# Row loads, small fills, a head pass and a last update, moved between engines in a hybrid decoder layer

## The chip, the cores and the metric

One core of one Trainium2 chip. The metric is the device time of one execution of the whole layer, in microseconds (us). The kernel before took 931.19 us, the median of three runs (928.84 to 931.49). Five engines run side by side, each through its own stream of instructions: TensorE (PE; its weight loads are shown apart, as PEld), VectorE (DVE), ScalarE (ACT), GpSimd (POOL) and SyncE (SP). SP issues DMAs only; ScalarE and GpSimd issue some too.

## The reference

One decoder layer over x of 1 x 512 x 1024 in float32. Two SwiGLU feed-forward blocks stand around a token mixer; each block is normed ahead and after.

```
x = x + 0.5 * rms_norm(swiglu_ffn(rms_norm(x, pre[0]), ffn1_w_in, ffn1_w_out), post[0])
mixed = token_mixer(rms_norm(x, pre[1]), w_mix_in, ...)     # HGRN2 heads and mLSTM heads
x = x + rms_norm(mixed, post[1])
x = x + 0.5 * rms_norm(swiglu_ffn(rms_norm(x, pre[2]), ffn2_w_in, ffn2_w_out), post[2])

def rms_norm(x, g):  return x * rsqrt(mean(x * x, axis=-1) + 1e-6) * g
def swiglu_ffn(x, w_in, w_out):
    gate, up = split(x @ w_in, 2)                           # 1024 -> 2 x 2816
    return (silu(gate) * up) @ w_out                        # 2816 -> 1024
```

The mixer reads one combined projection `h @ w_in`; its first four head tiles of 128 columns are the forget gates of the HGRN2 heads.

## The kernel before, in words

The 512 tokens are four tiles of 128 (i = 0 to 3), kept in `xs` (128 partitions x 4 x 1024). Every matmul operand is split into a high and a low part: ScalarE copies a float32 tile to fp32r (the high part, L289), VectorE subtracts it from the original (the low part, L291). A product is three passes: high weights by high x (0), high by low (1), low by high (2). Weights come by DMA in tiles of 512 KB into rings of raw buffers, a planner giving each load the product at whose split it is issued.

The stages in order of time: the start (0 to about 23 us), where x is loaded, normed and transposed; the first feed-forward, ended by `ffn_out` and `last`; the mixer, opened by `head4`; the second feed-forward; the stores.

**The start** (`layer`, `warm`, `gain_row`, `gain_pe`, `start`, `root_whole`) is traced under `manual_schedule`, so each engine keeps the written order there. L1903 loads x in halves of 256 KB: the second halves of tiles 0 and 1 from ScalarE's queue, all others from SP's. The norm row `norm_pre[0]` (2 KB in each half) is loaded by L176 into partition 0 of `self.row`, which lies in `hf`, after L171 has zeroed that half on VectorE. `gain_pe` (L183) spreads the row over the 128 partitions with a matmul by ones. `warm` and `spin` (L189) keep TensorE busy ahead of that. `root_whole` takes a tile's squares on ScalarE (L726) and the root on Pool (L727, and `pow` at L728). VectorE then multiplies by the row (L746) and by the root (L749), or both at once (L741). The results are transposed on TensorE (L359), copied by ScalarE (L379), and the first product (L614 in `prod`) begins. At L1910 ScalarE runs a tiny Exp, so that its table is loaded early.

**Small parameters** (`small_params`) follow the start in the source: among them are three Pool memsets, of `gb` (L1278, into which a DMA puts the gate biases), `tiny` (L1284) and `one` (L1286). Outside `manual_schedule` the framework orders each engine's stream itself by priority and dependencies; `with self.behind(a)` makes what is traced in its block on a's engine follow a. A PSUM bank is one of eight `ps` buffers; `holes` takes four without using them.

**The mixer's head** (`head4`, `head_mm`): `last` computes the last four chunks of the first feed-forward's output (L997), norms each (`post1`) and goes on to the mixer's pre-norm. `head4` splits weight tiles 0 to 3 and norms tiles 2 and 3 between them; then `head_mm` runs one weight tile over tokens 0 to 255 (L554, 24 matmuls: three passes of 8), and `trans(2)` and `trans(3)` (L359, then copies at L365 and L366) follow the second and the third tile. After the fourth, `forget_gates` runs the same four tiles over tokens 256 to 511 (L544).

**The end** (`last`, `post1`, `store`): for tile i, `post1` takes squares on ScalarE (L448), the root r on Pool (L449, L453), multiplies by the post-norm gain on VectorE (L496), and adds y * r and late * r to the two halves of `xs` on VectorE (L504). `store` writes each half from SP's queue (L1893).

Of the kernel before, what the change touches and what calls it, by code (L numbers as in the profile page):

```python
# [10 lines left out]
AF = mybir.ActivationFunctionType  # L11
ALU = mybir.AluOpType
PSUM = bass.MemoryType.PSUM

P = 128
T = 512
D = 1024
FF = 2816
NT = T // P
ND = D // P  # L20
# [4 lines left out]
HALF = T // 2  # L25
# [7 lines left out]
TINY = 1e-37  # L33
# [85 lines left out]
class Layer:  # L119
# [53 lines left out]

    def gain_row(self, row, h):
        v = slice(512 * h, 512 * h + 512)
        self.nc.sync.dma_start(self.row[0:1, v], row[:, v])  # L176

    def gain_pe(self):

# [309 lines left out]
    def post1(self, i, y, parts, rms, pieces, g, out=None):  # L489

        nc = self.nc
        for ps, v in pieces:
            parts.append(ps)
            next(rms)
            o = ps if out is None else out[:, v]
            nc.vector.tensor_tensor(o, ps, g[:, 512 + v.start : 512 + v.stop], op=ALU.mult)  # L496
        r = next(rms)

        late = (1, pieces[0][0] if out is None else out)
        turned, added = out is None and i == NT - 1, None  # L500
        for h, v in (late, (0, y)) if turned else ((0, y), late):
            x = self.xs[:, i, 512 * h : 512 * h + 512]
            with self.behind(*[added] * (turned and added is not None)):
                added = nc.vector.scalar_tensor_tensor(x, v, r, x, op0=ALU.mult, op1=ALU.add)  # L504
        self.added = [self.square, added]
# [40 lines left out]
                    start=k + n + m == 0, stop=k == ND - 1 and n == 2, skip_group_check=True,  # L546
                )

    def head_mm(self, w):

        ps = self.ps()
        for m, (a, b) in enumerate(((0, 0), (0, 1), (1, 0))):
            for k in range(ND):
                self.nc.tensor.matmul(  # L554
                    ps[:, :HALF], w[:, a, k, :], self.xop(k, b, 0, HALF), start=m + k == 0, stop=m == 2 and k == ND - 1
                )
        self.head.append((w, ps))

    def head4(self, trans, scaled):

        self.head = []
        lows = [self.low]
        self.full_split()
        with self.behind(*lows, self.low):
            scaled(2, 0)
        with self.behind(self.added[0]):
            self.full_split()
            with self.behind(self.low):  # L570
                scaled(2, 1)
            self.full_split()
        scaled(3, 0)
        scaled(3, 1)
        with self.behind(self.normed[1]):
            self.feed()
        for n in range(4):
            self.head_mm(self.pull())
            if n in (1, 2):
                trans(1 + n)  # L580

    def open_ffn(self, ctx, second=False):

# [137 lines left out]
    def root_whole(self, i):  # L721

        nc = self.nc
        out = self.hf[:, 2 * i : 2 * i + 2, :].rearrange("p a t -> p (a t)")
        ss, m, r = self.col(), self.col(), self.col()
        nc.scalar.activation(out, self.xs[:, i, :], AF.Square, accum_out=ss)  # L726
        nc.gpsimd.tensor_scalar(m, ss, 1.0 / D, EPS, op0=ALU.mult, op1=ALU.add)  # L727
        nc.gpsimd.tensor_tensor(r, m, self.nhalf[:, :1], op=ALU.pow)  # L728
        return r

    def start(self, gpre):
# [518 lines left out]
    def small_params(self):  # L1250

        nc = self.nc
        mc = self.cp
        rows = self.sp.tile([36, P], F32, tag="junk", bufs=1, name="rows")
        nc.sync.dma_start(rows[0:16, :], self.conv_w[0].rearrange("j (c p) -> (j c) p", p=P))
        nc.sync.dma_start(rows[16:20, :], self.conv_b[0].rearrange("(c p) -> c p", p=P))
        nc.sync.dma_start(rows[20:28, :], self.hgrn_lb_logits.rearrange("r (c p) -> (r c) p", p=P))
        nc.sync.dma_start(rows[28:32, :], self.hgrn_norm[0].rearrange("(c p) -> c p", p=P))
        nc.sync.dma_start(rows[32:36, :], self.mlstm_norm[0].rearrange("(c p) -> c p", p=P))
        pt = self.ps()  # L1260
        nc.tensor.transpose(pt[:, :36], rows, self.ident[:36, :36])
        nc.vector.tensor_copy(self.prm, pt[:, :36])
        l0, l1 = self.prm[:, 20:24], self.prm[:, 24:28]
        mx, e0, e1 = self.col(4), self.col(4), self.col(4)
        nc.vector.tensor_tensor(mx, l0, l1, op=ALU.max)
        nc.vector.tensor_tensor(e0, l0, mx, op=ALU.subtract)
        nc.vector.tensor_tensor(e1, l1, mx, op=ALU.subtract)
        nc.scalar.activation(e0, e0, AF.Exp)
        nc.scalar.activation(e1, e1, AF.Exp)
        nc.vector.tensor_tensor(e1, e0, e1, op=ALU.add)  # L1270
        nc.vector.reciprocal(e1, e1)
        self.lb = mc.tile([P, 4], F32, name="lb")
        nc.vector.tensor_tensor(self.lb, e0, e1, op=ALU.mult)
        self.oml = mc.tile([P, 4], F32, name="oml")
        nc.vector.tensor_scalar(self.oml, self.lb, -1.0, 1.0, op0=ALU.mult, op1=ALU.add)

        self.gb = mc.tile([36, 1], F32, name="gb")
        nc.gpsimd.memset(self.gb, 0.0)  # L1278
        bias = self.mlstm_gate_bias[0].rearrange("(g h) -> g h", g=2)
        for g in range(2):  # L1280
            nc.sync.dma_start(self.gb[32 * g : 32 * g + 4, :], bias[g].rearrange("(h o) -> h o", o=1))

        self.tiny = mc.tile([P, 1], F32, name="tiny")
        nc.gpsimd.memset(self.tiny, TINY)  # L1284
        self.one = mc.tile([P, 1], F32, name="one")
        nc.gpsimd.memset(self.one, 1.0)  # L1286

    def masks(self, mc, mb):

# [566 lines left out]
def layer(tc, aps):  # L1856
    with ExitStack() as ctx:
        L = Layer(ctx, tc, aps)
        nc = tc.nc
        x, out = aps["x"], aps["out"]  # L1860
        pre, post = aps["norm_pre"][0], aps["norm_post"][0]
        L.weights(
            L.ffn_items("f1", aps["ffn1_w_in"][0], aps["ffn1_w_out"][0]) + L.mix_items()
            + L.ffn_items("f2", aps["ffn2_w_in"][0], aps["ffn2_w_out"][0])
        )
        gp, xn, roots = [None], [None] * NT, {}

        def norm(i, row=None):
            if i == 0 and row is not None:
                gp[0] = L.gain("gpre", pre[row : row + 1, :])  # L1870
            xn[i] = L.pre(i, gp[0], row == 2 and i == NT - 1)

        def root(i):

            if i < 2:
                norm(i, 1)
            else:
                roots[i] = L.root(i)

        def scaled(i, h):  # L1880
            r, xn[i] = roots[i]
            L.scaled(i, gp[0], r, xn[i], h)

        def trans(i):
            L.to_t(i, xn[i])

        def trans_s(i):
            L.to_s(i, xn[i])

        def store(i):  # L1890
            for h in range(2):
                v = slice(512 * h, 512 * h + 512)
                nc.sync.dma_start(out[0, i * P : (i + 1) * P, v], L.xs[:, i, v])  # L1893

        with ExitStack() as f1:
            L.open_ffn(f1)
            with tc.manual_schedule():
                first = L.start_loads()
                L.warm()
                for i in range(NT):  # L1900
                    for h in range(2):
                        v = slice(512 * h, 512 * h + 512)
                        (nc.scalar if i < 2 and h else nc.sync).dma_start(L.xs[:, i, v], x[0, i * P : (i + 1) * P, v])  # L1903
                    if i < 2:
                        L.gain_row(pre[0:1, :], i)
                    if i:
                        L.load(first.popleft())
                    if i == 1:

                        nc.scalar.activation(L.col(), L.nhalf[:, :1], AF.Exp)  # L1910
                while first:
                    L.load(first.popleft())
                gp[0] = L.cp.tile([P, D], F32, tag="gpre", bufs=1, name=L.nm("gpre"))
                L.start(gp[0])
            L.small_params()
            L.ffn_in()
            L.ffn_out(post[0:1, :], 0.5, root, trans, lambda trans: L.head4(trans, scaled))
        L.mixer()
        with ExitStack() as f2:
            L.open_ffn(f2, True)  # L1920
            L.mix_out1(lambda i: norm(i, 2), trans_s, L.ffn_head)
            L.ffn_in()
            L.ffn_out(post[2:3, :], 0.5, store, lambda i: None, lambda trans: None)
# [30 lines left out]
```

## Time and profile before

| What | us |
|---|---|
| Median of three runs | 931.19 (928.84 to 931.49) |
| The profiled execution | 929.26 |
| Its span, first to last instruction | 927.6 |
| TensorE matmul busy | 917.6 |
| VectorE busy | 766.7 |
| ScalarE busy | 524.3 |
| GpSimd busy | 183.4 |

The profiled execution is one run; the profile's times count from the start of its span, and 1.66 us of its time lie outside the span. In a timeline row stand start, length, engine, source line, operation, output and inputs with their shapes, how many instructions the row merges (x), and in brackets the idle time of the engine just before, with what ended it. SPq and ACTq are DMA issues on those engines' queues. q1 in the DMA rows is SP's ring, q10 ScalarE's. The granted clock of TensorE was 0.999 of full speed.

### The profile page before, as it was taken

What the parts mean: (1) busy time and instruction counts of PE and PEld (TensorE: products, weight loads), DVE (VectorE), ACT (ScalarE), POOL (GpSimd) and SP (SyncE); (2) the same over time, 40 slices, a digit from 0 to 9 for tenths busy, and PEclk for the clock granted to TensorE, in tenths of its full rate; (3) what the DMA queues carried; (4) which work ended last, traced back from release to release, by engine and by line L of the source; (5) the groups of instructions that cost most, each with busy time, mean ns of one, the idle gap of its engine ahead of it and who ended that gap; (6) DMA issues with size and microseconds to landing.
All of it is one profiled execution on the core that took longest, in us unless ns stands there. A gap on an engine that the chain in (4) does not pass through costs nothing.

```text
span 927.6 us, 18301 instructions
## 1 busy us (share of the span) xinstructions
PE 917.6 (99%) x7425; PEld 883.9 (95%) x7425; DVE 766.7 (83%) x994; ACT 524.3 (57%) x751; POOL 183.4 (20%) x252
## 2 busy tenths in 40 slices
PE   8999999999999999999999999999999999999997
PEld 7999999999999999998888887899999999999997
DVE  6899988889887876698767555699898889998885
ACT  7645455557566466956533345595354545756661
POOL 2431112111111046652220310314000000011002
PEclk9999999999999999999999999999999999999999
DMA  9255878766897824898832124262354435278542
GB/s 315 73 165 131 190 206 197 191 151 159 222 282 226 246 79 131 170 196 185 171 75 70 46 92 155 96 183 70 113 160 137 137 115 160 93 218 259 174 144 92
DMA packets 118768, 145.42 MB, mean 157 GB/s; under 512 B 7414, under 2 KB 91418, under 8 KB 118684
## 3 DMA queue, kind: packets, MB, share of 16 engines
q1 hardware_dynamic: 102716, 129.05, 45.2%
q0 software_dynamic: 15680, 14.69, 12.0%
q8 instruction: 58, 0.95, 0.4%
q10 hardware_dynamic: 288, 0.52, 0.2%
q14 instruction: 26, 0.21, 0.1%
HBM read 142.14 MB, written 31.46 MB: 187 GB/s over the span
## 4 chain that ended last, share of the span: by engine, by line
PE 59%; DVE 2%; DMA 1%; issue 1%; ACT 1%; POOL 0%; DVEq 0%; POOLq 0%; ACTq 0%
PE ps L614 19%; PE ps L1005 8%; PE ps L544 6%; PE ps L193 5%; PE ps L195 5%; PE ps L194 5%; PE ps L997 4%; PE ps L1423 2%; DMA raw<-in_ffn_w_in_dram 1%; DVE w L291 1%; PE ps L359 1%; PE ps L554 1%; PE ps L1516 0%; PE ps L1721 0%; PE ps L1694 0%
## 5 line engine op out<-in xcount | busy, mean ns | idle before, releaser
L289 ACT CAST w<-raw 128x1024 fp32r<-128x1024 f32 x246 | 251.1, 1027 | 196.4 <-PE ps L614 95.8
L291 DVE TENSOR_TENSOR w<-raw,w 128x1024 fp32r<-128x1024 f32 x246 | 299.3, 1220 | 30.6 <-ACT w L289 28.5
L614 PE MATMUL ps<-xq,w 128*128 128x256 f32 x2016 | 237.1, 277 | 0.0
L614 PEld LDWEIGHTS ps<-xq,w 128*128 128x128 f32 x2016 | 232.9, 188 | 0.0
L614 PE MATMUL ps<-sq,w 128*128 128x256 f32 x1512 | 178.0, 276 | 0.6 <-DVE ps L633 0.3
L614 PEld LDWEIGHTS ps<-sq,w 128*128 128x128 f32 x1512 | 174.3, 188 | 1.4 <-ACT ps L665 0.9
L305 DVE TENSOR_TENSOR raw<-raw,raw 128x1024 f32<-128x1024 f32 x72 | 89.9, 1252 | 8.1 <-DMA raw<-in_ffn_w_in_dram 6.6
L1005 PE MATMUL ps<-w,hs 128*128 128x256 f32 x672 | 81.0, 276 | 0.0
L997 PE MATMUL ps<-w,hs 128*128 128x256 f32 x672 | 79.2, 276 | 0.0
L1005 PEld LDWEIGHTS ps<-w,hs 128*128 128x128 f32 x672 | 78.4, 188 | 0.0
L193 PE MATMUL ps<-w,xq 128*128 128x512 f32 x192 | 77.9, 407 | 0.1
L997 PEld LDWEIGHTS ps<-w,hs 128*128 128x128 f32 x672 | 77.5, 188 | 0.0
L194 PE MATMUL ps<-w,xq 128*128 128x512 f32 x192 | 74.8, 391 | 0.0
L195 PE MATMUL ps<-w,xq 128*128 128x512 f32 x192 | 74.8, 391 | 0.0
L544 PE MATMUL ps<-xq,w 128*128 128x256 f32 x480 | 55.8, 277 | 0.0
L544 PEld LDWEIGHTS ps<-xq,w 128*128 128x128 f32 x480 | 54.9, 188 | 0.5 <-issue 0.5
L937 POOL DMA_DIRECT2D f2sums<-in_ffn_w_out_dram x15 | 20.3, 1502 | 176.9 <-DMA f2sums<-in_ffn_w_out_dram 176.6
L877 ACT CAST hs<-hf 128x1024 fp32r<-128x1024 f32 x32 | 33.7, 1053 | 28.9 <-PE ps L1005 21.2
L878 DVE TENSOR_TENSOR hs<-hf,hs 128x1024 fp32r<-128x1024 f32 x32 | 39.1, 1222 | 8.8 <-ACT hs L877 8.2
L193 PEld LDWEIGHTS ps<-w,xq 128*128 128x128 f32 x192 | 36.1, 188 | 8.4 <-issue 1.0
L937 POOL DMA_DIRECT2D f1sums<-f1sums x26 | 22.3, 857 | 110.2 <-DMA f1sums<-in_ffn_w_out_dram 58.2
L195 PEld LDWEIGHTS ps<-w,xq 128*128 128x128 f32 x192 | 36.0, 188 | 8.1 <-DVE xq L366 0.3
(275 smaller groups left out, 1215.8 us busy)
## 6 DMA issues: line engine op xcount, KB each, us to landing
raw<-in_ffn_w_in_dram SPq DMA_DIRECT2D x98, 512.0 KB, 5.5
raw<-in_ffn_w_out_dram SPq DMA_DIRECT2D x44, 512.0 KB, 4.5
raw<-in_w_mix_in_dram SPq DMA_DIRECT2D x28, 512.0 KB, 5.9
raw<-f2sums SPq DMA_DIRECT2D x15, 512.0 KB
raw<-f1sums SPq DMA_DIRECT2D x13, 512.0 KB, 7.0
raw<-in_w_mix_out_dram SPq DMA_DIRECT2D x8, 512.0 KB, 3.8
f2sums<-in_ffn_w_out_dram SPq DMA_DIRECT2D x30, 128.0 KB, 6.3
f2sums<-in_ffn_w_out_dram SPq DMA_DIRECT2D x15, 256.0 KB, 4.5
```

The costliest lines, as they stand in the source:

```text
L193: mm(ps, sh, mh, start=start, stop=False, **kw)
L194: mm(ps, sh, ml, start=False, stop=False, **kw)
L195: mm(ps, sl, mh, start=False, stop=stop, **kw)
L289: nc.scalar.copy(hi, raw)
L291: self.low = nc.vector.tensor_tensor(lo, raw, hi.bitcast(F32), op=ALU.subtract)
L305: added = (nc.vector if late else nc.gpsimd).tensor_tensor(o, o, c, op=ALU.add)
L544: mm(ps[:, u0:u1], w[:, a, k, :], self.xop(k, b, u0, u1), start=k + n + m == 0, stop=k == ND - 1 and n == 2, skip_group_check=True,)
L614: self.nc.tensor.matmul(ps[:, c], wb[b][:, k, v], left[d][:, k, :], start=first and a + n + k == 0, stop=n == 2 and k == KH - 1, skip_grou ...
L878: self.nc.vector.tensor_tensor(lo, src, hi.bitcast(F32), op=ALU.subtract)
L937: nc.gpsimd.dma_start(to[:, a:b], v, accum_op=ALU.add)
L997: mm(out, a[kk][:, i * P : (i + 1) * P], w[:, b, kk, QUARTER * v : QUARTER * (v + 1)], start=begin and c == kk == n == 0, stop=kk == 1 and ...
L1005: mm(ps[:, QUARTER * c : QUARTER * (c + 1)], A[a][:, c], B[b], start=begin and c == n == 0, stop=n == 2, skip_group_check=True,)
```

## The change

Four edits. **Rows:** the two norm-row DMAs are issued from ScalarE's queue; row 0 is traced ahead of x, row 1 after x[1]. The second half of x[0] moves to SP's queue, so that ScalarE's holds row 0, the second half of x[1], row 1. **Fills:** the three Pool memsets of `small_params` stand behind the `pow` of the start's last root. **Head:** `head_pass` does one pass of one tile, and the third tile's pass 0 is run between the second tile's passes 1 and 2; `trans(2)` still follows the second tile's last pass and `trans(3)` the third's. **Last update:** for the last token tile of the second feed-forward, ScalarE multiplies the upper 256 columns of `out` by r, VectorE updates columns 0 to 511 and 512 to 767, and Pool adds columns 768 to 1023; that tile is stored in three pieces, the last of them from ScalarE's queue.

```diff
     def gain_row(self, row, h):
         v = slice(512 * h, 512 * h + 512)
-        self.nc.sync.dma_start(self.row[0:1, v], row[:, v])
+        self.nc.scalar.dma_start(self.row[0:1, v], row[:, v])
...
         late = (1, pieces[0][0] if out is None else out)
+        if self.second and out is not None and i == NT - 1:
+            x = self.xs[:, i, :]
+            nc.scalar.activation(out[:, 256:], out[:, 256:], AF.Copy, scale=r)
+            for a, b, v in ((0, 512, y), (512, 768, out[:, :256])):
+                nc.vector.scalar_tensor_tensor(x[:, a:b], v, r, x[:, a:b], op0=ALU.mult, op1=ALU.add)
+            nc.gpsimd.tensor_tensor(x[:, 768:], x[:, 768:], out[:, 256:], op=ALU.add)
+            return
...
-    def head_mm(self, w):
-
-        ps = self.ps()
-        for m, (a, b) in enumerate(((0, 0), (0, 1), (1, 0))):
-            for k in range(ND):
-                self.nc.tensor.matmul(
-                    ps[:, :HALF], w[:, a, k, :], self.xop(k, b, 0, HALF), start=m + k == 0, stop=m == 2 and k == ND - 1
-                )
-        self.head.append((w, ps))
+    def head_pass(self, t, m):
+
+        if t == len(self.head):
+            self.head.append((self.pull(), self.ps()))
+        (w, ps), (a, b) = self.head[t], ((0, 0), (0, 1), (1, 0))[m]
+        for k in range(ND):
+            self.nc.tensor.matmul(
+                ps[:, :HALF], w[:, a, k, :], self.xop(k, b, 0, HALF), start=m + k == 0, stop=m == 2 and k == ND - 1
+            )
...
-        for n in range(4):
-            self.head_mm(self.pull())
-            if n in (1, 2):
-                trans(1 + n)
+        for t, m in ((0, 0), (0, 1), (0, 2), (1, 0), (1, 1), (2, 0), (1, 2), (2, 1), (2, 2), (3, 0), (3, 1), (3, 2)):
+            self.head_pass(t, m)
+            if (t, m) in ((1, 2), (2, 2)):
+                trans(1 + t)
...
-        nc.gpsimd.tensor_tensor(r, m, self.nhalf[:, :1], op=ALU.pow)
+        self.pow = nc.gpsimd.tensor_tensor(r, m, self.nhalf[:, :1], op=ALU.pow)
         return r
...
-        nc.gpsimd.memset(self.gb, 0.0)
+        with self.behind(self.pow):
+            nc.gpsimd.memset(self.gb, 0.0)
...
         self.tiny = mc.tile([P, 1], F32, name="tiny")
-        nc.gpsimd.memset(self.tiny, TINY)
         self.one = mc.tile([P, 1], F32, name="one")
-        nc.gpsimd.memset(self.one, 1.0)
+        with self.behind(self.pow):
+            nc.gpsimd.memset(self.tiny, TINY)
+            nc.gpsimd.memset(self.one, 1.0)
...
         def store(i):
-            for h in range(2):
-                v = slice(512 * h, 512 * h + 512)
-                nc.sync.dma_start(out[0, i * P : (i + 1) * P, v], L.xs[:, i, v])
+            for q, a, b in [(nc.sync, 0, 512)] + [(nc.sync, 512, D)] * (i < 3) + [(nc.sync, 512, 768), (nc.scalar, 768, D)] * (i == 3):
+                q.dma_start(out[0, i * P : (i + 1) * P, a:b], L.xs[:, i, a:b])
...
                 for i in range(NT):
+                    if i == 0:
+                        L.gain_row(pre[0:1, :], 0)
                     for h in range(2):
                         v = slice(512 * h, 512 * h + 512)
-                        (nc.scalar if i < 2 and h else nc.sync).dma_start(L.xs[:, i, v], x[0, i * P : (i + 1) * P, v])
-                    if i < 2:
-                        L.gain_row(pre[0:1, :], i)
+                        (nc.scalar if i == h == 1 else nc.sync).dma_start(L.xs[:, i, v], x[0, i * P : (i + 1) * P, v])
+                    if i == 1:
+                        L.gain_row(pre[0:1, :], 1)
```

## The prediction

> **What bounds the kernel now.** I read the page first, then the table by stages, and then the order of time at the three places that the diff touches.
>
> ```profile
> span 927.6 us, 18301 instructions
> ...
> PE 917.6 (99%) x7425; PEld 883.9 (95%) x7425; DVE 766.7 (83%) x994; ACT 524.3 (57%) x751; POOL 183.4 (20%) x252
> ```
>
> TensorE is busy for 917.6 of 927.6 us, so 10.0 us in all is not matmul time. An edit that takes no matmul away can win only from those ten, or from weight loads that stall inside a stage. The table by stages (stretch, length, then busy us of each engine) says where they lie.
>
> ```profile
> 0.00:23.20 23.20, 20.79 (x145) 18.21 (x146) 16.07 (x23) 17.81 (x29) 5.51 (x20) 1.00 0.95 316
> ...
> 336.00:352.00 16.00, 15.80 (x136) 15.40 (x135) 13.71 (x19) 9.52 (x20) 8.37 (x10) 1.00 0.62 186
> ...
> 921.20:927.60 6.40, 0.00 (x0) 0.00 (x0) 2.31 (x5) 0.43 (x2) 0.81 (x2) 0.87 0.44 164
> ```
>
> The start holds 2.41 us without a matmul (23.20 less 20.79), the head of the mixer 0.20, the tail 6.40. Together that is 9.0 of the 10.0, and all four edits sit in these three stretches. The start's matmuls are partly warm-up, so what counts there is when the first real product (L614) begins. These are its rows in order of time (start, length, engine, line):
>
> ```profile
> 0.79 0.89 ACTq L1903 DMA_DIRECT2D xs<-in_x_dram  x2
> ...
> 0.80 0.39 SPq L1903 DMA_DIRECT2D xs<-in_x_dram  x1
> ...
> 0.97 1.02 DVE L171 MEMSET hf<- 128x512 f32 x2 [0.97 <-PEq L1941]
> ...
> 1.48 0.31 SPq L176 DMA_DIRECT2D hf<-in_norm_pre_dram  x1
> ...
> 4.62 1.06 ACT L726 ACTIVATE hf<-xs 128x1024 f32<-128x1024 f32 x1 [1.42 <-DMA xs<-in_x_dram]
> ...
> 4.86 2.24 PE L183 MATMUL ps<-hf,ones 128*128 128x512 f32 x4 [0.70 <-DMA hf<-in_norm_pre_dram]
> ...
> 6.11 0.09 POOL L1278 MEMSET gb<- 36x1 f32 x1
> ...
> 6.22 1.06 ACT L726 ACTIVATE hf<-xs 128x1024 f32<-128x1024 f32 x1 [0.45 <-DMA xs<-in_x_dram]
> 6.24 0.56 POOL L728 TENSOR_TENSOR col<-col,nhalf 128x1 f32<-128x1 f32 x1
> ...
> 6.60 0.68 DVE L746 TENSOR_TENSOR hf<-xs,ps 128x512 f32<-128x512 f32 x1
> ...
> 7.20 0.48 DVE L749 TENSOR_SCALAR xn<-xn,col 128x512 f32<-128x512 f32 x1
> ...
> 7.81 0.56 POOL L728 TENSOR_TENSOR col<-col,nhalf 128x1 f32<-128x1 f32 x1
> ...
> 8.40 0.49 DVE L749 TENSOR_SCALAR hf<-hf,col 128x512 f32<-128x512 f32 x1
> 8.43 0.58 ACT L379 CAST xq<-ps 128x512 fp32r<-128x512 f32 x1 [1.05 <-PE ps L359]
> ...
> 9.86 1.57 ACT L379 CAST xq<-ps 128x512 fp32r<-128x512 f32 x3
> ...
> 10.50 5.91 PE L614 MATMUL ps<-xq,sq 128*128 128x256 f32 x48 [0.23 <-ACT xq L379]
> ```
>
> Read backwards: the product at 10.50 waits for ScalarE's copy at 9.86 (tile 1), which stands behind the copy at 8.43 (tile 0) and one weight copy. The copy at 8.43 waits for transposes behind VectorE's L749 at 7.20. That one had its root (6.24 + 0.56 = 6.80) long before; it waits for VectorE's two L746, and these for the row's broadcast at 4.86, which waits for the row's DMA. So the row's landing is the start of the chain of tile 0. Tile 1 has a second one: x lands at 6.22, root at 7.81 + 0.56 = 8.37, L749 at 8.40.
>
> **The change part by part: the rows on ScalarE's queue.** Row 0 must wait for its memset on either queue: two memsets fill 0.97 to 1.99, the first ends at 1.48, and the row is issued there. The new queue issues it no earlier. What changes is the ring it stands in. Before, row 0 lies behind x[0]'s first half in SP's ring; afterwards it is first in ScalarE's. The packets of ScalarE's ring (q10) and SP's (q1) show that the ring with the row falls behind; this is 3.5 to 4.0 us:
>
> ```profile
> q10 hardware_dynamic: 66, 0.12, 70.8%
> q1 hardware_dynamic: 18, 0.02, 13.3%
> ```
>
> x[0] was issued at 0.80 and is used at 4.62, 3.8 us for 512 KB over two rings. Row 0 took 4.86 - 1.48 = 3.4 us, almost all of it in line. Alone at the head of its ring I put it at 2.4 us, between the 0.8 us from issue to first data at the end of the run (below) and 3.4; it lands at about 3.9. The warm-up matmuls then hold TensorE to about 4.2, so the broadcast comes some 0.65 us earlier. For that, x[0]'s second half moves behind its first on SP, 0.39 later in issue, while x[1]'s second half waits on ScalarE's queue behind the row (from 1.24 to about 1.8). x[0] is then served before x[1] instead of beside it. I let x[0] land 0.15 later (bounds: 0.4 earlier, 0.4 later), so its root would end at 6.95, and without the three **Pool memsets** (6.11 to 6.24, 0.13 us) at 6.82. These go behind the last root of the start, where the first reader is a bias DMA on SP's queue microseconds later: nothing there is late. So tile 0's L749 moves from 7.20 to about 6.87, and the copy at 8.43 to 8.1. Then the next thing is late: tile 1. Its x lands with the same megabyte, at about 6.2, L749 stays at 8.4, its transposes end near 9.6, and the copy that stood at 9.86 starts at about 9.63. That is **-0.23 us**, and no more, however early the row. Behind the rows on ScalarE's queue stands its table load; it moves from 1.71 to about 2.6 and ends at 3.9, under the 4.62 at which ScalarE is first needed. Row 1 now stands behind half of x[1] in ScalarE's ring; if that costs it 0.4, the gain becomes a loss of 0.2. Ends kept: -0.4 and +0.3.
>
> The Trainium skill, "DMA: Bandwidth & Descriptors", section "Issuing engines are not separate DMA queues", speaks against this: all rings run on the same 16 DMA engines, so a second issuing engine saves issue time only. By that rule alone this term would be nothing, and the sum -0.3. The trace agrees for the megabyte of x, not for the row, whose place in line is what I count.
>
> **The third head tile's first pass.** The mixer's head, same columns:
>
> ```profile
> 338.75 4.62 PEld L554 LDWEIGHTS ps<-xq,w 128*128 128x128 f32 x40 [0.29 <-ACT w L289]
> ...
> 339.15 1.99 ACT L289 CAST w<-raw 128x1024 fp32r<-128x1024 f32 x2
> ...
> 342.40 1.22 DVE L291 TENSOR_TENSOR w<-raw,w 128x1024 fp32r<-128x1024 f32 x1
> ...
> 343.67 0.98 PEld L554 LDWEIGHTS ps<-xq,w 128*128 128x128 f32 x8 [0.31 <-DVE w L291]
> ...
> 344.19 1.22 DVE L291 TENSOR_TENSOR w<-raw,w 128x1024 fp32r<-128x1024 f32 x1
> ...
> 348.68 2.48 DVE L366 TENSOR_TENSOR xq<-ps,xq 128x512 fp32r<-128x512 f32 x4
> ...
> 351.89 20.25 PEld L544 LDWEIGHTS ps<-xq,w 128*128 128x128 f32 x178
> ```
>
> 40 loads (five passes of 8, 0.1155 us each) end at 343.37. The sixth pass needs the second tile's low part, which VectorE gives at 343.62: 0.31 us of stall. The third tile's high part has been there since 341.14 (339.15 + 1.99), so its first pass, 8 x 0.1155 = 0.92 us, covers the hole, and the sixth pass then finds its weights ready. What is late next? Tile 2's transposes come 0.92 - 0.31 = 0.6 us later, at 345.2. They feed VectorE's L366, which does not start before 348.68 because it stands behind another L291, so that costs nothing. Passes two and three of the third tile need its low part at 344.19 + 1.22 = 345.41 and come at 346.1. L544 begins at 351.6 and reads first what the third L366 writes, at about 350.5. The whole hole goes: **-0.31 us**, and with TensorE full behind it, it stays. Bounds -0.35 and +0.8 (a weight split of 1.22 us slipping ahead of L366, less the 0.4 us of slack).
>
> **The last update.** Tile 3's rows at the end, then what DMA moved from 923.6 in steps of 0.1 us, then rows for prices:
>
> ```profile
> 922.73 0.75 DVE L504 SCALAR_TENSOR_TENSOR xs<-y,col,xs 128x512 f32<-128x512 f32 x1 [0.63 <-POOL col L453]
> 923.39 0.75 DVE L504 SCALAR_TENSOR_TENSOR xs<-hf,col,xs 128x512 f32<-128x512 f32 x1
> 923.50 0.33 SPq L1893 DMA_DIRECT2D out_dram<-xs  x1
> ```
>
> ```profile
> GB/s 0 0 0 0 0 0 0 205 348 451 389 369 328 369 369 389 410 389 389 369 369 103 0 0 0 0 0 0 0 0 0 0 0 0 0 0 0 0 0 0
> ```
>
> ```profile
> 25.21 2.41 POOL L305 TENSOR_TENSOR raw<-raw,raw 128x1024 f32<-128x1024 f32 x1
> ...
> 26.84 1.87 DVE L291 TENSOR_TENSOR w<-raw,w 128x1024 fp32r<-128x1024 f32 x1 [0.25 <-ACT w L289]
> ```
>
> ```profile
> L294 ACT ACTIVATE w<-raw,prm x16: 710/726/766, 528.4 to 576.7; 128x512 fp32r<-128x512 f32 x16
> ```
>
> VectorE's second half of the update falls from 0.75 to about 0.42 (half the columns), while ScalarE scales 256 columns in about 0.47 (from 0.726 for 512), ready at 923.2. Pool then adds 256 columns: a quarter of 2.41 is 0.60, with a start I take 0.7 (bounds 0.6 and 1.0). But Pool and VectorE do not run side by side here: L291, 1.22 us long elsewhere, took 1.87 while Pool's L305 ran to 27.62, so one waits for the other. The 0.42 and the 0.7 follow the first L504 one after the other, and the last piece is ready near 924.5 instead of 924.14. The Trainium skill, "SBUF — State Buffer", section "Who interferes with whom", says the same as a rule: a VectorE instruction with two SBUF inputs and a GpSimd instruction that reads SBUF exclude each other. By it, too, the update ends later, not earlier.
>
> The store hides that. The two stores of tile 3 flow without a gap from 924.33 to 925.75 at about 370 GB/s, and the first starts where it did. 512 KB at that rate end at 925.75 whatever the pieces. The last piece is 128 KB (0.35 us of flow), so it may be issued as late as 925.75 - 0.35 - 0.83 = 924.57 (0.83 from the issue at 923.50 to the data at 924.33). Ready near 924.5 is just in time: **0.0 us**, bounds -0.3 and +0.5.
>
> **Sum.** -0.23 - 0.31 + 0.0 is about -0.55 us. The profiled execution took 929.26 us, 1.66 more than its span, and would take 928.7. The median of the runs is 931.19, but this execution and the lowest run (928.84) lie 2 us under it; all four average 930.2, and I forecast 930.2 - 0.6 = **929.6**.
>
> **The rivals.** *Rows gain nothing* (tile 1 alone decides, or the skill's rule on issuing engines holds fully): -0.3, 929.9. For it: tile 1's rows above. *The tail costs*: Pool's add goes second and takes 1.0, so the store is issued at 924.9, +0.35; the sum is -0.2, 930.0. *Slower, at VectorE's queue in the head*: outside the start the framework orders each engine's stream itself, and the memsets at 6.11, written after the start's code, show that it moves things. If splits (L291, 1.22 each) slip ahead of L366, L544 waits. The first costs 0.8, each further one 1.22; it decides from the point where the third L366 ends after 351.6. Three give +3.2, less 0.23: 933.2. Against it: the splits are held in place in the source. *Faster*: SP's ring, freed of the rows, brings x[1] 0.8 us earlier, and two queues end the stores 0.4 earlier: -1.0 - 0.3 - 0.4 = -1.7, 928.5, or -0.3% against the median shown.
>
> **How the numbers follow.** 0.3% (2.8 us) is about what a measurement of this kernel can tell from no change. Forecast 0.56, rows nothing 0.14, tail 0.08: these three are within it, 0.78. Faster 0.13, slower 0.09. The range takes the executions' own spread (928.84 to 931.49) less 0.6, the open ends of the terms (-1.05 and +1.6), and most of the faster case; it leaves out the slower one: 927.3 to 932.3.
>
> **What would show it.** Right: the row's broadcast near 4.2, L614 at 10.2 to 10.3, no stall in L554's weight loads before the sixth pass, L544 at 351.3 (both gains), Pool's add lengthened or behind VectorE's L504, data of the last store ending as long after L504's start as now. Wrong: a broadcast that still waits for the second row; L366 behind more than one L291; a last store later than 924.6 on this scale; or a shift of over 1 us in stages that no edit touches.

## The result and the profile after

The changed kernel is slower. Its median is 932.99 us (932.09 to 934.08, 8 runs) against 930.45 us for the kernel before, run beside it (928.84 to 931.49, 8 runs): a ratio of 1.0028, 95% interval 1.0017 to 1.0039, or +2.54 us. The forecast was 929.6, a gain of 0.6. The profiled execution of the changed kernel took 933.30 us, 4.04 more than that of before, so what the two traces show is not all the change; part of it is chance, and the experiments have to say which part.

The page after has the span and the busy time of each engine:

```profile
span 931.6 us, 18305 instructions
...
PE 921.0 (99%) x7425; PEld 887.0 (95%) x7425; DVE 767.2 (82%) x994; ACT 525.1 (56%) x752; POOL 184.4 (20%) x253
```

TensorE has the same 7425 matmuls as before and is busy for 3.4 us longer (921.0 against 917.6). So most of the loss is not waiting: the same matmuls take longer. An argument from idle time alone, such as the forecast's "ten us in all is not matmul time", cannot see that.

**The start**, in order of time (start, length, engine, line; the lines of before stand 7 to 10 lines further down from L500 on, since the change adds lines):

```profile
1.49 0.51 ACTq L176 DMA_DIRECT2D hf<-in_norm_pre_dram  x1
2.03 0.39 ACTq L1913 DMA_DIRECT2D xs<-in_x_dram  x1
...
2.46 0.29 ACTq L176 DMA_DIRECT2D hf<-in_norm_pre_dram  x1
...
4.03 2.05 PE L183 MATMUL ps<-hf,ones 128*128 128x512 f32 x2
...
4.59 1.06 ACT L733 ACTIVATE hf<-xs 128x1024 f32<-128x1024 f32 x1 [0.31 <-DMA xs<-in_x_dram]
...
6.10 0.55 POOL L735 TENSOR_TENSOR col<-col,nhalf 128x1 f32<-128x1 f32 x1
...
6.99 2.04 PE L183 MATMUL ps<-hf,ones 128*128 128x512 f32 x2 [0.92 <-DMA hf<-in_norm_pre_dram]
...
7.55 1.06 ACT L733 ACTIVATE hf<-xs 128x1024 f32<-128x1024 f32 x1 [1.81 <-DMA xs<-in_x_dram]
...
9.07 0.75 DVE L748 SCALAR_TENSOR_TENSOR xn<-xs,col,ps 128x512 f32<-128x512 f32 x1 [0.65 <-PE ps L183]
...
12.85 1.42 PE L621 MATMUL ps<-xq,sq 128*128 128x256 f32 x10 [0.77 <-ACT xq L379]
```

Row 0 does land earlier: its broadcast begins at 4.03 instead of 4.86. But tile 1's x is squared at 7.55 instead of 6.22, and row 1's broadcast (two of the four L183 matmuls) begins at 6.99 and waits for the row's DMA. The first product begins at 12.85, 2.35 us later than before.

**The mixer's head**, TensorE's weight loads, first after, then before:

```profile
341.01 6.44 PEld L562 LDWEIGHTS ps<-xq,w 128*128 128x128 f32 x56 [0.29 <-ACT w L289]
...
350.14 0.90 PEld L359 LDWEIGHTS ps<-ident,hf 128*128 128x128 f32 x8
351.01 2.89 PEld L562 LDWEIGHTS ps<-xq,w 128*128 128x128 f32 x24
353.83 33.99 PEld L551 LDWEIGHTS ps<-xq,w 128*128 128x128 f32 x288
...
392.57 14.79 PEld L551 LDWEIGHTS ps<-xq,w 128*128 128x128 f32 x125 [0.24 <-issue]
407.29 2.53 PEld L1432 LDWEIGHTS ps<-qe,ke 128*72 128x72 f32 x32
```

```profile
345.45 2.89 PEld L554 LDWEIGHTS ps<-xq,w 128*128 128x128 f32 x24
...
349.16 2.81 PEld L554 LDWEIGHTS ps<-xq,w 128*128 128x128 f32 x24
351.89 32.72 PEld L544 LDWEIGHTS ps<-xq,w 128*128 128x128 f32 x288
...
389.41 14.26 PEld L544 LDWEIGHTS ps<-xq,w 128*128 128x128 f32 x125 [0.24 <-issue]
403.60 2.53 PEld L1423 LDWEIGHTS ps<-qe,ke 128*72 128x72 f32 x32
```

The hole of 0.31 us is gone: 56 loads run without a break from 341.01. The shift against before falls from 2.26 us at the head's first load (341.01 less 338.75) to 1.94 at the first load of `forget_gates` (353.83 less 351.89). Then the same 288 loads, in the same order, take 33.99 us instead of 32.72: 0.1180 us each instead of 0.1136. No row of the stream waits for another engine; the 0.24 us ahead of the 125 stands in both. The next 125 lose another 0.53 us. Behind them the shift is 3.69 us (407.29 less 403.60), so it has grown by 1.75 us since the first load of `forget_gates`, in a stage that no edit touches. The 24 loads ahead of the 288 already run slowly (2.89 us against 2.81); that loss is already in the 1.94.

**The last update**, after, and Pool's last root before:

```profile
926.00 0.55 POOL L453 TENSOR_TENSOR col<-col,nhalf 128x1 f32<-128x1 f32 x1
926.58 0.51 ACT L502 ACTIVATE hf<-hf,col 128x256 f32<-128x256 f32 x1 [1.10 <-POOL col L453]
926.58 0.75 DVE L504 SCALAR_TENSOR_TENSOR xs<-y,col,xs 128x512 f32<-128x512 f32 x1 [0.63 <-POOL col L453]
927.17 0.75 POOL L505 TENSOR_TENSOR xs<-xs,hf 128x256 f32<-128x256 f32 x1 [0.62 <-ACT hf L502]
927.25 0.95 DVE L504 SCALAR_TENSOR_TENSOR xs<-hf,col,xs 128x256 f32<-128x256 f32 x1
```

```profile
922.14 0.55 POOL L453 TENSOR_TENSOR col<-col,nhalf 128x1 f32<-128x1 f32 x1
```

VectorE's piece of 256 columns takes 0.95 us while Pool's add runs beside it from 927.17 to 927.92; it ends 0.28 us after Pool does. The update is whole 1.62 us after its first L504 began (928.20 less 926.58); before, with two pieces of 512 columns on VectorE alone, after 1.41 us (924.14 less 922.73). From Pool's last root to the end of the span it is 5.6 us (931.6 less 926.00) against 5.5 (927.6 less 922.14). With the trace's unrounded ends, 931.59 and 927.55, it is 5.59 against 5.41: the tail lost 0.18 us. It is no accident of one execution: from the last square on ScalarE to the end of the span the three profiles with this edit have 6.57 to 6.59 us, the eleven without it 6.40 to 6.42.

So there are three places: the start (+2.35 us in these two executions), the head and the stream behind it (-0.32, then +1.75), and the tail (+0.18).

### The profile page after: what moved, and what is told of

Read it like the earlier page. It is cut to its first block, busy times and chain, and to the rows that moved or that the text cites. A ratio compares the mean times of both kernels' runs of the same rounds, so it can differ in the third digit from the quotient of the medians.

```text
span 931.6 us, 18305 instructions
## 1 busy us (share of the span) xinstructions
PE 921.0 (99%) x7425; PEld 887.0 (95%) x7425; DVE 767.2 (82%) x994; ACT 525.1 (56%) x752; POOL 184.4 (20%) x253
## 4 chain that ended last, share of the span: by engine, by line
PE 59%; DVE 2%; DMA 1%; issue 1%; ACT 1%; DVEq 0%; POOL 0%; ACTq 0%; POOLq 0%
PE ps L621 19%; PE ps L1012 8%; PE ps L551 6%; PE ps L193 5%; PE ps L195 5%; PE ps L194 5%; PE ps L1004 4%; PE ps L1432 2%; PE ps L562 1%; DMA raw<-in_ffn_w_in_dram 1%; DVE w L291 1%; PE ps L359 1%; PE ps L1525 0%; PE ps L1730 0%; PE ps L1703 0%
```

## The experiments

Four theories were tried. A: the moved loads make the start slower. B: the head's new order makes TensorE slower behind it. C (a form of B): the stream of 128-column loads has two rates, 113.3 and 117.7 ns, and which one holds is settled when it is entered behind the transposes. D: when the start's first product begins hangs on when TensorE's full clock is granted, which differs between executions of one program. The first four kernels ran on one chip, the next four on a second, the last four on a third, each group beside runs of the kernel before.

**The two kernels again**, unchanged, one execution each.

> The kernel before once more, for a second profile of the same program. Both theories: the first real product (L614) again between 10.3 and 10.7 us and TensorE's full clock granted near 4.3 us, if these belong to the program. If they belong to the single execution, the product moves by up to 2 us and the grant by up to 3.4 us with nothing changed.

> The changed kernel once more. Theory A (the loss is in the start, made by the moved loads): the first product again at 12.5 to 13.2 us, x[1] and row 1 landing near 7 us, and no slower matmuls between 350 and 410 us, since those (118 ns for each weight load instead of 113) would belong to that one execution. Theory B (the head's new order slows TensorE behind it): the 118 ns are there again in the same stretch.

Measured: 930.75 us for before and 932.36 for after. The slow stream came back in after (33.99 us for the 288 loads), not in before. The first product of after began at 11.33, earlier than the 12.5 that theory A asked for at least. But the first product of before, the same program, began at 12.47 instead of 10.50:

```profile
4.91 3.75 PE L183 MATMUL ps<-hf,ones 128*128 128x512 f32 x4 [0.74 <-DMA hf<-in_norm_pre_dram]
8.45 1.06 PE L189 MATMUL ps<-ones 128*128 128x128 f32 x4
9.30 1.60 PE L359 MATMUL ps<-ident,xn 128*128 128x128 f32 x8
10.74 1.04 PE L359 MATMUL ps<-ident,hf 128*128 128x128 f32 x8
12.47 0.74 PE L614 MATMUL ps<-xq,sq 128*128 128x256 f32 x4 [0.69 <-ACT xq L379]
```

The four broadcast matmuls begin 0.05 us later than in the first profile and take 3.75 us instead of 2.24. They ran at the low clock. The trace's record of the full clock begins at 4.31 us in the first profile, at 10.45 here, and at 10.66 in the profile of after. So up to 1.97 of the 2.35 us in the start can come without the edit. All kernels with the old loads and the old warm-up, some of which follow below, fall into one line (full clock, then first product): 4.31 and 10.50, 4.48 and 10.51, 8.43 and 11.61, 9.17 and 11.93, 9.66 and 12.22, 9.81 and 12.32, 10.45 and 12.47. The later the grant, the later the product. The records of the full clock also differ in length by multiples of 3.41 us (925.01, 921.60, 918.19, 914.77). The Trainium skill, "TensorE: Matmul & The Clock Gate", section "Part 1: The HAM clock gate (the "warmup" mystery)", says that the monitor behind the clock looks at a free-running window of 3.4 us, which does not begin with the kernel. The steps of 3.41 us agree. The page gives about 0.5 us to either side for the start of the full clock by this window; here the two starts of one program lie 6.14 us apart (4.31 and 10.45), so the window alone does not explain them. What puts the grant off is not shown.

**The loads alone, and all but the loads** (theory A against B).

```diff
 # loads_only: the kernel before, with
-        self.nc.sync.dma_start(self.row[0:1, v], row[:, v])
+        self.nc.scalar.dma_start(self.row[0:1, v], row[:, v])
...
+                    if i == 0:
+                        L.gain_row(pre[0:1, :], 0)
...
-                        (nc.scalar if i < 2 and h else nc.sync).dma_start(L.xs[:, i, v], x[0, i * P : (i + 1) * P, v])
-                    if i < 2:
-                        L.gain_row(pre[0:1, :], i)
+                        (nc.scalar if i == h == 1 else nc.sync).dma_start(L.xs[:, i, v], x[0, i * P : (i + 1) * P, v])
+                    if i == 1:
+                        L.gain_row(pre[0:1, :], 1)
 # no_loads: the kernel after, with these lines undone
```

> The kernel before with the moved row and x loads alone. Theory A: as slow as the changed kernel or 0.2 slower, +2.1 to +2.8 us (ratio 1.0023 to 1.0030), first product near 12.8 us. Theory B: no more than +0.5 us.

> The changed kernel with row and x loads back as they were; fills, head and last update stay changed. Theory A: first product at 10.4 to 10.6 us, the head 0.3 us shorter, the tail 0.1 us longer, in all -0.2 us (ratio 0.9995 to 1.0003). Theory B: +1.5 to +2 us, and 118 ns for a weight load between 350 and 410 us.

Measured: loads_only 931.57 us against 930.82, ratio 1.0012 (1.0002 to 1.0021); no_loads 933.05, ratio 1.0021 (1.0013 to 1.0030). Both theories hold a part. The loads alone cost about 0.75 us by the medians, 1.1 by the ratio (0.2 to 2.0 by its interval), instead of gaining 0.23; theory A's +2.1 is missed. The rest of the change costs about 2.2 us. In the profiles the first product began at 12.23 with the moved loads (full clock from 6.41) and at 12.22 without them (from 9.66, a row of the list above). The slow stream is in no_loads (33.99 us for the 288 loads) and not in loads_only (32.71).

**The head's order alone, and what of it does it** (theories B and C). Four kernels, all the kernel before but for the head; only the lines that matter are shown:

```diff
 # head_only: the new order and nothing else of the change
+        for t, m in ((0, 0), (0, 1), (0, 2), (1, 0), (1, 1), (2, 0), (1, 2), (2, 1), (2, 2), (3, 0), (3, 1), (3, 2)):
+            self.head_pass(t, m)
+            if (t, m) in ((1, 2), (2, 2)):
+                trans(1 + t)
 # bank_only: the old order, but the third tile's PSUM bank is taken before trans(2), as in the new one
+            if n == 1:
+                self.head.append((self.pull(), self.ps()))
+                self.head.append((self.pull(), self.ps()))
 # head_t3late: the new order, with trans(3) one pass later
+            if (t, m) in ((1, 2), (3, 0)):
+                trans(2 if t == 1 else 3)
 # head_dummy: the new order, and behind trans(3) one product of ident by itself,
 # into columns of the fourth tile's bank that are written again later
+            if (t, m) == (2, 2):
+                self.head.append((self.pull(), self.ps()))
+                self.nc.tensor.matmul(self.head[3][1][:, HALF : HALF + P], self.ident, self.ident, start=True, stop=True)
```

> The kernel before with the head's new order of passes alone. Theory C (seen in three traces with that order: behind the transposes of tile 3 TensorE's stream runs at 117.7 ns for a weight load instead of 113.3, and keeps that for 50 us): the stall of 0.31 us is gone, the stretch from 351 to 407 us loses 1.8 to 1.9 us, net +1.5 us (ratio 1.0010 to 1.0022). Rival (the slow stretch belongs to the other edits or to the execution): -0.3 us and 113.3 ns throughout.

> The old order of passes, but the third tile's PSUM bank taken ahead of the transposes of tile 2, as the new order takes it. Theory C (the rate is set when the stream starts again behind the transposes, by what ran ahead of them): 113.3 ns behind tile 3's transposes, as before. Rival (the changed banks make TensorE slower): 117.7 ns from 349 to 407 us.

> The new order, with tile 3's transposes one pass of eight matmuls later (behind the fourth tile's first pass), so that 24 matmuls stand between the two groups of transposes, as before the change, and not 16. Theory C: the stream's rate behind the transposes can come out other than in the new order; 113.3 ns if the number of matmuls between the transposes decides. Rival (anything that runs with the third tile's pass early): 117.7 ns as in the changed kernel.

> The new order with one extra 128x128 matmul of the identity by itself, into a part of the fourth tile's bank that is overwritten later, between tile 3's transposes and the fourth tile's product (about 0.4 us more work). Theory C: the stream starts from another place and can fall into the 113.3 ns rate; then the net is about 0 to +0.2 us. If the slow rate stays: +1.9 us. Rival (banks or addresses): 117.7 ns, +1.9 us.

| Kernel | Matmuls between the transposes | Time, us | Before beside it | Ratio (95%) | 288 loads, us |
|---|---|---|---|---|---|
| head_only | 16 | 932.40 | 930.61 | 1.0018 (1.0009 to 1.0027) | 33.99 |
| bank_only | 24, old order | 930.85 (one execution) | 930.61 | | 32.71 |
| head_t3late | 24, new order | 930.64 (one execution) | 930.61 | | 32.72 |
| head_dummy | 16, and the extra product | 930.63 | 930.61 | 0.9996 (0.9987 to 1.0005) | 32.72 |

These are weight loads of head_only and of head_dummy:

```profile
348.12 0.90 PEld L359 LDWEIGHTS ps<-ident,hf 128*128 128x128 f32 x8
348.99 2.89 PEld L555 LDWEIGHTS ps<-xq,w 128*128 128x128 f32 x24
351.81 33.99 PEld L544 LDWEIGHTS ps<-xq,w 128*128 128x128 f32 x288
```

```profile
349.62 0.90 PEld L359 LDWEIGHTS ps<-ident,hf 128*128 128x128 f32 x8
350.49 0.30 PEld L583 LDWEIGHTS ps<-ident 128*128 128x128 f32 x2
350.71 2.81 PEld L555 LDWEIGHTS ps<-xq,w 128*128 128x128 f32 x24
353.45 32.72 PEld L544 LDWEIGHTS ps<-xq,w 128*128 128x128 f32 x288
```

One added product (two loads and two matmuls in the records, which put the stream off by 0.22 us) between the transposes and the stream brings 24 loads from 2.89 to 2.81 and 288 from 33.99 to 32.72 us. It takes away 1.77 us of the median (932.40 less 930.63). The granted clock is not the cause; here is the stretch from 352 to 407 us (busy time and number of each engine, then granted clock, DMA share and GB/s), in head_only and in head_dummy:

```profile
352.00:407.00 55.00, 55.00 (x474) 54.52 (x473) 39.65 (x58) 43.94 (x50) 33.21 (x50) 1.00 0.76 153
```

```profile
352.00:407.00 55.00, 55.00 (x491) 54.52 (x489) 39.62 (x59) 43.83 (x49) 34.89 (x51) 1.00 0.74 149
```

The clock is 1.00 and TensorE is busy for all 55 us in both; it gets through 474 matmuls in the one and 491 in the other. VectorE, ScalarE, Pool and DMA do about the same in both. The choice of the PSUM bank is not it either (bank_only is fast). The slow stream stands at this place in all four profiles of the three kernels that have the new order and nothing behind it (after in two executions, no_loads, head_only), and in none of the ten others. The cleanest pair of profiles is head_only and before. Their first products began at 10.51 and 10.50 us and the head's first load at 338.75 in both; behind the 125 loads head_only is 1.67 us late (405.27 less 403.60). (Of this, 0.58 us is made up further on, at places that no edit touches, and that execution of 930.36 us was head_only's fastest.)

So it is shown that the order sets the rate at this place. The number of matmuls between the transposes does not decide it alone: head_dummy has 16 and is fast. Nor does one kernel have one rate; it can change in either direction where other loads come between. In before, the 24 loads between the two groups of transposes ran slowly (2.89 us), and in all fourteen profiles the stretch at that place did. The 18 loads between the 288 and the 125 took 2.19 us in before and 2.13 in after. Elsewhere the order of the code does not settle it: the last 174 loads of the run had the slow rate in again_after, x_only and spin8, some 0.7 us, and the fast one in after, which is the same program as again_after. What in TensorE holds the rate is not shown: no row tells the two streams apart but by their spacing.

**The rows alone, and the move of x alone** (why theory A's loss).

```diff
 # rows_only: as loads_only, but x[0]'s second half stays on ScalarE's queue, so both halves there stand behind row 0
 # x_only: the kernel before, with
-                        (nc.scalar if i < 2 and h else nc.sync).dma_start(L.xs[:, i, v], x[0, i * P : (i + 1) * P, v])
+                        (nc.scalar if i == h == 1 else nc.sync).dma_start(L.xs[:, i, v], x[0, i * P : (i + 1) * P, v])
```

> The kernel before with the two norm rows on ScalarE's queue (row 0 first, row 1 last), and both second halves of x[0] and x[1] still there too. If the rows' place makes the loss: x[1] is squared at 7.2 to 8.2 us instead of 6.2 to 6.6, and row 1's broadcast begins at 6.6 or later. If the move of x[0]'s second half to SP's queue makes it: x[1] at 6.2 to 6.7 us.

> The kernel before with x[0]'s second half moved to SP's queue and the rows left on SP's queue. If that move makes the loss: x[1] is squared at 7.2 to 8.2 us. If the rows' place does: x[1] at 6.2 to 6.7 us.

Measured, one execution each: rows_only 933.95 us, x_only 930.76, beside 931.02 for before. The start of rows_only:

```profile
1.49 0.52 ACTq L176 DMA_DIRECT2D hf<-in_norm_pre_dram  x1
...
2.04 0.85 ACTq L1905 DMA_DIRECT2D xs<-in_x_dram  x2
...
7.39 1.06 ACT L726 ACTIVATE hf<-xs 128x1024 f32<-128x1024 f32 x1 [2.63 <-DMA xs<-in_x_dram]
...
9.00 1.06 ACT L726 ACTIVATE hf<-xs 128x1024 f32<-128x1024 f32 x1 [0.46 <-DMA xs<-in_x_dram]
...
9.31 2.05 PE L183 MATMUL ps<-hf,ones 128*128 128x512 f32 x2 [3.44 <-DMA hf<-in_norm_pre_dram]
...
15.20 0.96 PE L614 MATMUL ps<-xq,sq 128*128 128x256 f32 x6 [0.24 <-ACT xq L379]
```

Both tiles now have a half that stands behind row 0 in ScalarE's queue. It is issued at 2.04 instead of 0.79, because row 0 at the queue's head waits until 1.49 for its memset; and both tiles are squared 2.8 us later than in before (7.39 against 4.62, 9.00 against 6.22). 1.25 us later at the issue became 2.8 us later at the use. Row 1 came late as well, and its broadcast at 9.31 is what VectorE waited for last. The full clock came late here too (14.13), so not all of the 15.20 is the loads'. In x_only nothing on ScalarE's queue stands behind a row, and tile 1 is squared at 6.80, just outside the 6.2 to 6.7 expected; row 0's broadcast began at 5.46, and the first product at 11.09 with the full clock from 4.65, 0.59 after the first profile of before. Whether the move of x costs something by itself is not shown by this: in spin8 below, whose loads are those of before, the broadcast began at 5.50 and the first product at 11.14.

How the two rings share the transfer from 5.0 to 5.5 us, first after, then before (q10 is ScalarE's ring, q1 SP's):

```profile
DMA packets 70, 0.11 MB, mean 217 GB/s; under 512 B 6, under 2 KB 28, under 8 KB 70
...
q10 hardware_dynamic: 31, 0.06, 44.5%
q1 hardware_dynamic: 39, 0.05, 30.8%
```

```profile
DMA packets 118, 0.17 MB, mean 338 GB/s; under 512 B 12, under 2 KB 59, under 8 KB 118
...
q1 hardware_dynamic: 116, 0.17, 90.5%
q10 hardware_dynamic: 2, 0.00, 1.5%
```

Before, ScalarE's ring is done by then; after, it still brings x[1]'s half, and the whole moves at 217 GB/s instead of 338. Why the ring with the row at its head flows so slowly is not settled. One thing changed with it and was not tried by itself: without the rows, SP's queue issues the first weights at 2.17 us instead of 2.56 and the next two halves of x at 2.65 instead of 2.99, and from 3.5 to 4.0 us SP's ring moved 57 packets and ScalarE's 3 (before, 18 and 66).

**A longer warm-up, and the best of all** (theory D).

```diff
 # spin8: the kernel before, with
-        self.spin(6, self.ones)
+        self.spin(8, self.ones)
 # best: that, and the head of head_dummy; loads, memsets and last update as before
```

> The kernel before with eight warm-up calls instead of six, so that the warm-up runs on until row 0 has landed (16 matmuls of 0.21 us from 1.23 us). Theory D (the start's time hangs on when TensorE's full clock is granted, and a gap ahead of the broadcast often puts that off to 8 to 10.5 us): the grant comes by 8.1 us, the first product at 10.5 to 11.6, and the median is 0.4 to 1.0 us lower (ratio 0.9989 to 0.9996). Rival (the grant falls where it falls): no change, the first product anywhere from 10.5 to 12.5.

> The kernel before with eight warm-up calls, the head's new order and the one extra matmul behind tile 3's transposes; loads, fills and last update as before. Theories C and D: 113.3 ns from 351 to 407 us and the first product at 10.5 to 11.6 us, 0.5 to 1.2 us under the kernel before (ratio 0.9987 to 0.9995). Rivals: no change.

Measured: spin8 930.14 us against 931.02, ratio 0.9991 (0.9982 to 1.0000, so no change is not excluded); best 929.44, ratio 0.9984 (0.9975 to 0.9993). Best is faster than the kernel before by 1.6 us, and its runs lie closer together (928.75 to 930.43 in 11 runs, against 929.44 to 933.81 in 21). Here is the start of best:

```profile
4.81 3.02 PE L183 MATMUL ps<-hf,ones 128*128 128x512 f32 x4
7.67 0.61 PE L189 MATMUL ps<-ones 128*128 128x128 f32 x4
...
11.29 0.97 PE L617 MATMUL ps<-xq,sq 128*128 128x256 f32 x6 [0.40 <-ACT xq L379]
```

In best the two more spins (four matmuls in the records) fill the 0.7 us in which TensorE waited ahead of the broadcast: the row of L183 has no idle time in brackets any more. In spin8 they did not: row 0 came later, and TensorE waited 0.59 us until 5.50. The full clock began at 7.08 in best and at 4.68 in spin8, and the first product at 11.29 and 11.14, between the 10.50 and 12.47 of before. That is what theory D expected, but with two profiled executions it is not shown that the late grant is excluded. That a gap ahead of the broadcast puts the grant off is not shown either: with gaps of 0.70, 0.71 and 1.29 us in before, head_only and x_only the grant came at 4.31, 4.48 and 4.65. That best gains 0.7 us over spin8 lies in two groups of runs whose spreads overlap, and is not separated.

## Why the prediction was wrong, point by point

**The base was right.** 930.2 us was taken for the kernel before; its median beside the changed one was 930.45.

**The head is the step that failed most.** The forecast was -0.31 us, "and with TensorE full behind it, it stays". The hole did go, by 0.32 us, and the queue that the slower rival feared did nothing: the four L366 after follow their split in one run, and TensorE reaches `forget_gates` without a wait. But it did not stay. A full TensorE was taken for one with a fixed price per matmul. The stream behind the new order runs at 0.1180 us a load instead of 0.1136 and gives back 1.75 us. With head_only the edit costs 1.79 us in the median.

**The start had the wrong sign.** The forecast was -0.23 us. Row 0's landing was right (broadcast "near 4.2": 4.03 to 4.33 in the three profiles with both moves), and x[0] was within its bounds (squared at 4.38 to 4.59, against 4.77 forecast). The step that failed is tile 1: "Its x lands with the same megabyte, at about 6.2, L749 stays at 8.4". It was squared at 7.35 to 8.25 in these three profiles; with the old loads it was at 6.18 to 6.59 in eight profiles and at 7.20 in one (no_loads). In again_after and loads_only VectorE then waits 0.56 us for tile 1's root, so tile 1 is what comes last there. The working saw that x[1]'s half waits behind the row, from 1.24 to about 1.8, and charged only that half a microsecond of issue, hidden by the shared engines; the issue was at 2.03, and the landing moved by more than the issue. The open end for row 1 (+0.3) named the right queue and, in these two profiles, the wrong load. At like starts of the full clock the price is +0.83 us (again_after 11.33 with 4.12, before 10.50 with 4.31) and +0.38 (after 12.85 with 10.66, again_before 12.47 with 10.45); the median of loads_only says +0.75. A pair of profiles says little here, since spin8, with the old loads, began at 11.14 with 4.68.

**The Pool memsets cost nothing, as said.** They stand behind the start's last root, and nothing there waits for them in the trace; no run has them alone:

```profile
20.38 1.41 POOL L735 TENSOR_TENSOR col<-col,nhalf 128x1 f32<-128x1 f32 x1
21.75 0.09 POOL L1286 MEMSET gb<- 36x1 f32 x1
```

The root of tile 0 comes without the memsets ahead of it, at 6.10 instead of 6.24, and gains nothing either: VectorE's chain for that tile is later.

**The tail cost 0.18 us, not 0.0.** That VectorE and Pool exclude each other agrees with the trace: one of the two pieces took 0.95 us beside Pool's add instead of the 0.42 expected. No run has that piece without the add. The last piece was ready 1.62 us after the first L504, sooner than the forecast's 1.77 (924.5 less 922.73). What failed is "the store hides that". The trace's last packet came 3.20 us after the first L504 instead of 3.12, and the span ended 0.1 us later still behind it, with three stores on two queues instead of two on one. Which of the two queues adds this was not tried.

**The sum.** The forecast's -0.23, -0.31 and 0.0 stand against these: loads +0.75 and head +1.79 by their medians, tail +0.18: +2.7, against +2.54 measured, each of the first two with an interval of about 0.9 us to either side. The rival that ended slower gave 933.2, near the 932.99 measured, but by a mechanism that did not occur; the near hit is chance. Of the signs listed as wrong, the last one came true: a shift of over 1 us in a stage that no edit touches.

## What to carry to other kernels

Where TensorE is busy for 99% of the span, compare the time of equal runs of matmuls as well as the idle time: an edit of the order can cost more in the rate behind it than the hole that it fills. A small load that waits, put at the head of a queue, delays all that stands behind it, so ask first what the queue's next transfer is worth. Before two profiles are compared at the start, read how long equal matmuls take in each, since the same program here began its first product at 10.50 and at 12.47 us.

## What the runs showed of the hardware that was not expected

- A stream of equal 128 x 128 loads and 256-column matmuls, at a granted clock of 1.00, has two rates, 0.1136 and 0.1180 us a load (32.72 and 33.99 us for 288). In after it kept the slower one over 288 loads and, behind 18 faster loads, again over 125. One extra product that put the stream off by 0.22 us set the faster one.
- The full clock was granted between 4.1 and 14.1 us after the start of the span in the fourteen profiled executions, and the first product of one and the same program moved by 1.97 us with it. Much of the spread of before's runs (2.6 to 4.4 us in the four groups) can be this.
- A VectorE instruction of 256 columns took 0.95 us beside a Pool add of 0.75 us; one of 512 columns just ahead of it took 0.75.
